# Gated linear attention, output stage: two heads on the partitions, both directions in the free dimension, and masks applied by one multiplication

## The chip, the cores and the metric

The kernel runs on one core of a Trainium2 chip. The metric is device time in microseconds (us), the median of three runs. The engines are called as in the profile: PE (TensorE), DVE (VectorE), ACT (ScalarE), POOL (GpSimd) and SP (SyncE, which issues the DMAs).

## The reference

Two layers over 2048 latent tokens and 256 context tokens, model width 1024. Layer 0 has latent attention and an mLSTM; layer 1 has a bidirectional gated linear attention (GLA, 4 heads, key width 64, value width 128) and a 2-D neighbourhood attention (8 heads). The change touches the GLA alone. For one head and one direction, cut to what matters:

```python
bcum = jnp.cumsum(gc, axis=2)                      # gc: log decay per token and key channel
rel = bcum[:, :, :, None, :] - bcum[:, :, None, :, :]
decay = jnp.exp(jnp.where(causal[:, :, None], rel, -jnp.inf))
att = jnp.einsum('bhtd,bhsd,bhtsd->bhts', qc, kc, decay)
o = att @ vc + (qc * jnp.exp(bcum)) @ S            # S: state before the chunk
```

The second direction runs over the flipped sequence, and the outputs of both directions are added. Then a per-head RMS norm follows.

## The kernel before

Layer 1 first makes one projection, a long row of f16 products on PE (`gemm_in`: L322 with 384 columns where tokens stand in the columns, L343 with 256 columns where they stand on the rows). It is split into parts, and the parts of the GLA are written between them: gates (`gla_gates`, L1126), chunk states (`gla_state`, L1186), projection of q, `gla_out` (L1262), the projection for the neighbourhood attention, and that attention (`na_attn`). A scheduler orders each engine's instructions for the whole program before it is built; each engine then runs its list in order. So the products of the projection stand between the products of `gla_out`, and fill PE while the GLA waits.

`gla_out` goes over 16 chunks of 128 tokens. The decay between two tokens of a chunk is not formed token by token. For block sizes hb = 64, 32, 16 (HIGH) and 8, 4, 2, 1 (LOW), `decay` subtracts from the summed log decay its value at the middle of each block of 2·hb tokens (`Dt`, POOL, L1301), and takes the exponential of both halves with opposite signs (`E`, ACT, L1303 and L1304, into PSUM). Queries of one half times keys of the other half, each multiplied by `E`, then give the products between the two halves of a block.

The partitions hold direction times 64 key channels, and the free dimension holds the 4 heads. So one direction's queries are the first half of a block and the other's are the second half, on other partitions, and each level needs `queries` twice with 64 partitions (DVE, L1308, L1309), and for HIGH also the keys twice (L1321, L1322). For LOW the keys are multiplied whole (L1333), and `R` and `Sb` hold zeros where nothing may count. HIGH products are added up in one PSUM tile, `pb` (L1327). LOW products go to places of their own (`pl`, L1342) in 32 by 32 blocks, the diagonal too (L1344, in a second tile `o`). ACT copies `pb` to `att` and the first LOW level to `ac`. DVE then takes from each level what its mask allows:

```python
nc.vector.copy_predicated(ac, mkc[:, li - 1, None, :]..., pc[:, li] if li < len(LOW) else o[:, :, 0:32])
nc.vector.copy_predicated(att, mkx[...], ac[...])
```

Last come `att` times `v` (L1355) and the queries `qe` times the state `Z` (L1356), the squares for the norm on ACT (L1358), a copy (`ob`, L1360) and a store. `E` has two buffers in PSUM, `pb` and `o` share two, `pl` has one.

A float32 product of the program is two matmuls in the trace. A product with 32 or 64 output rows takes only a strip of PE's array: the forms 128\*32 and 128\*64 in the profile are rows times columns of the part of the array that is used.

Of the kernel before, what the change touches and what calls it, by code (L numbers as in the profile page):

```python
# [7 lines left out]
F32 = mybir.dt.float32  # L8
# [4 lines left out]
U32 = mybir.dt.uint32  # L13
AF = mybir.ActivationFunctionType
ALU = mybir.AluOpType
AX = mybir.AxisListType
PSUM = bass.MemoryType.PSUM
# [41 lines left out]
class Kern:  # L59
# [1066 lines left out]
    def gla_gates(self, kp):  # L1126
# [4 lines left out]
        with tc.tile_pool(name="gl_gc", bufs=1, side="right") as gc, tc.tile_pool(name="gl_g", bufs=2, side="right") as gp, \  # L1131
# [24 lines left out]
            for g in (0, 2):  # L1156
# [11 lines left out]
                for a in range(2):  # L1168
# [6 lines left out]
                    nc.sync.dma_start(S["glB"][:, h], Fp[:, h])  # L1175
# [86 lines left out]
    def gla_out(self):  # L1262
        nc, tc, I, S = self.nc, self.tc, self.I, self.S
        HIGH, LOW = (64, 32, 16), (8, 4, 2, 1)
        with ExitStack() as es:
# [5 lines left out]
            pl = mk(name="gl_pl", bufs=1, space=PSUM)  # L1271
            po = mk(name="gl_po", bufs=2, space=PSUM)
            mkc = cp.tile([P, 4, 32], F32, name="mkc")
            nc.sync.dma_start(mkc, I["lmaskc"].rearrange("l s t -> s l t"))
            mkx = cp.tile([P, 4, 32], F32, name="mkx")
            nc.sync.dma_start(mkx, I["lmaskx"].rearrange("s (n t) -> s n t", t=32))
            Sb = cp.tile([P, len(HIGH), 4, P], F32, name="Sb")
            nc.gpsimd.memset(Sb, 0.0)
            R = []
            for i in range(2):  # L1280
                r = cp.tile([P, len(HIGH + LOW), 4, P], F32, name=f"R{i}")
                nc.gpsimd.memset(r, 0.0)
                R.append(r)
            def load(c):
                cs = slice(c * P, (c + 1) * P)
                t = [lp.tile([P, 4, P], F32, name=n, bufs=b) for n, b in (("B", 3), ("q", 2), ("k", 2), ("v", 2), ("Z", 3))]
                B, q, k, v, Z = t
                nc.sync.dma_start(B, S["glB"][:, :, cs])
                for r in (0, 64):
                    nc.sync.dma_start(k[r:r + 64], S["gk"][:, cs].rearrange("(h p) t -> p h t", p=64))  # L1290
                    nc.sync.dma_start(q[r:r + 64], S["gq"][:, cs].rearrange("(h p) t -> p h t", p=64))
                nc.sync.dma_start(v, S["gva"][cs, 0:512].rearrange("p (h d) -> p h d", h=4))
                nc.sync.dma_start(Z[0:64], S["glZ"][c, 0:64])
                nc.sync.dma_start(Z[64:128], S["glZ"][NT + 1 - c, 64:128])
                return t

            def decay(hb, B):
                F = lambda t: t.rearrange("p h (n x) -> p (h n) x", x=2 * hb)
                V = lambda t: t.rearrange("p h (n s b) -> p (h n) s b", s=2, b=hb)
                Dt = wp.tile([P, 4, P], F32, name="Dt")  # L1300
                nc.gpsimd.tensor_tensor(F(Dt), F(B), F(B)[:, :, hb:hb + 1].broadcast_to([P, 4 * P // (2 * hb), 2 * hb]), ALU.subtract)  # L1301
# [3 lines left out]
                return V, E  # L1305

            def queries(V, E, q, r):
                nc.vector.tensor_tensor(V(r)[0:64, :, 1], V(E)[0:64, :, 1], V(q)[0:64, :, 1], ALU.mult)  # L1308
                nc.vector.tensor_tensor(V(r)[64:128, :, 0], V(E)[64:128, :, 0], V(q)[64:128, :, 0], ALU.mult)  # L1309

            order = [c for i in range(NT // 2, 1, -1) for c in (i, NT + 1 - i)]
            nxt = load(order[0])
            for i, c in enumerate(order):
                B, q, k, v, Z = nxt
                nxt = load(order[i + 1]) if i + 1 < len(order) else None
                Rc = R[c % 2]
                pb = po.tile([P, 4, P], F32, name="o")
                for li, hb in enumerate(HIGH):
                    V, E = decay(hb, B)
                    Sv = V(Sb[:, li])  # L1320
                    nc.vector.tensor_tensor(Sv[0:64, :, 0], V(E)[0:64, :, 0], V(k)[0:64, :, 0], ALU.mult)  # L1321
                    nc.vector.tensor_tensor(Sv[64:128, :, 1], V(E)[64:128, :, 1], V(k)[64:128, :, 1], ALU.mult)  # L1322
                    queries(V, E, q, Rc[:, li])
                    for h in range(4):
                        for n in range(P // (2 * hb)):
                            w = slice(n * 2 * hb, (n + 1) * 2 * hb)
# [469 lines left out]
```

## Time and profile before

| what | us |
| --- | --- |
| median of 3 runs | 3649.45 (3647.62 to 3654.1) |
| the profiled execution | 3645.0 |
| its span, first to last instruction | 3642.7 |
| PE busy | 3391.9 (93%) |
| DVE busy | 2563.9 (70%) |
| ACT busy | 1832.6 (50%) |
| POOL busy | 972.9 (27%) |

The span leaves 2.3 us of the profiled execution around it. Busy time counts an engine as busy from the start to the end of each instruction. Matmuls are pipelined, and the next begins before the last has ended, so for PE the distance between starts says more than the durations. A wait is put down to the instruction whose signal came last.

### The profile page before, as it was taken

The numbers are of one execution on the slowest core, as the hardware profiler recorded it, in microseconds if no ns is written. First come the engines' busy times: TensorE is split into PE (matmuls) and PEld (weight loads), VectorE is DVE, ScalarE is ACT, GpSimd is POOL, SyncE is SP. The second block draws the span as 40 slices with busy tenths as digits, with TensorE's granted clock in tenths as the row PEclk, the third lists the DMA queues.
The fourth block names the chain that finished last, engine by engine and source line by source line (L and its number), as shares of the span: only waits on it lengthen the run. The fifth ranks groups of instructions, "written<-read, shape, count | busy, mean of one in ns | idle before, by whom it ended". The sixth has DMA issues, their size and how long they took to land.

```text
span 3642.7 us, 77364 instructions
## 1 busy us (share of the span) xinstructions
PE 3391.9 (93%) x30588; PEld 2575.3 (71%) x30588; DVE 2563.9 (70%) x5697; ACT 1832.6 (50%) x3243; POOL 972.9 (27%) x908
## 2 busy tenths in 40 slices
PE   6999999999888899999999999999888899899898
PEld 3566888898556677777777555676565789898754
DVE  5657576678766888888887566354688547776887
ACT  4333323334443577777777433256465435455632
POOL 1012204473221233333333222101355322111122
PEclk8999999999999799999999999999999999999999
DMA  7632347776778222221110543227554545437343
GB/s 264 242 122 69 141 179 227 222 234 218 215 225 231 77 49 52 53 49 47 31 47 14 168 152 121 66 83 211 166 160 133 144 98 145 123 96 194 117 164 122
DMA packets 400535, 498.35 MB, mean 137 GB/s; under 512 B 104110, under 2 KB 306339, under 8 KB 394988
## 3 DMA queue, kind: packets, MB, share of 16 engines
q1 hardware_dynamic: 400172, 493.40, 44.7%
q8 instruction: 241, 3.95, 0.5%
q14 instruction: 122, 1.00, 0.1%
HBM read 311.73 MB, written 181.43 MB: 135 GB/s over the span
## 4 chain that ended last, share of the span: by engine, by line
PE 58%; DVE 20%; DMA 12%; issue 5%; ACT 4%; POOL 1%; SPq 1%; POOLq 0%; DVEq 0%; ACTq 0%
PE ps L343 13%; PE ps L322 8%; PE po L633 5%; PE ops L1119 4%; PE pm L578 4%; PE ps L613 3%; PE ps L615 3%; PE ps L614 3%; PE t L1544 2%; DVE mc L579 1%; PE s L1522 1%; PE o L1560 1%; PE s L1523 1%; DMA scr_mqkc<-y 1%; PE ps L489 1%
## 5 line engine op out<-in xcount | busy, mean ns | idle before, releaser
L343 PE MATMUL ps<-wh,uh 128*128 128x256 f16 (+3 forms) x2816 | 742.6, 269 | 33.8 <-ACT ot L278 13.0
L343 PE MATMUL ps<-wl,uh 128*128 128x256 f16 (+3 forms) x2816 | 741.6, 268 | 0.0
L343 PE MATMUL ps<-wh,ul 128*128 128x256 f16 (+3 forms) x2816 | 736.3, 268 | 1.4 <-POOL ul L210 1.4
L343 PEld LDWEIGHTS <-uh 128*128 128x128 f16 x5632 | 532.1, 99 | 118.2 <-issue 43.4
L579 DVE TENSOR_REDUCE mc<-pm 128x1 f32<-128x512 f32 (+1 forms) x656 | 403.2, 628 | 115.5 <-PE pm L578 107.3
L618 ACT ACTIVATE p<-ps 128x1024 f32<-128x1024 f32 (+1 forms) x296 | 299.8, 1013 | 158.8 <-PE ps L615 119.2
L322 PE MATMUL ps<-uh,wh 128*128 128x384 f16 (+2 forms) x1008 | 323.9, 325 | 7.5 <-DVE ofs L332 2.8
L322 PE MATMUL ps<-ul,wh 128*128 128x384 f16 (+2 forms) x1008 | 326.1, 326 | 1.1 <-DVE ul L210 1.1
L322 PE MATMUL ps<-uh,wl 128*128 128x384 f16 (+2 forms) x1008 | 325.7, 325 | 0.0
L622 POOL TENSOR_TENSOR pl<-p,ph 128x1024 f16<-128x1024 f32 (+1 forms) x98 | 207.9, 2122 | 434.8 <-ACT ph L619 416.5
L619 ACT CAST ph<-p 128x1024 f16<-128x1024 f32 (+1 forms) x296 | 306.4, 1035 | 7.6
L343 PEld LDWEIGHTS <-ul 128*128 128x128 f16 x2816 | 277.6, 99 | 37.7 <-POOL ul L210 2.6
L322 PEld LDWEIGHTS <-wh 128*128 128x128 f16 (+1 forms) x2016 | 198.2, 100 | 134.8 <-issue 24.0
L578 PE MATMUL pm<-kk,qq 96*128 96x512 f32 (+1 forms) x656 | 271.5, 418 | 21.4 <-DVE mc L579 15.8
L622 DVE TENSOR_TENSOR pl<-p,ph 128x1024 f16<-128x1024 f32 (+1 forms) x198 | 244.4, 1236 | 27.7 <-ACT ph L619 23.0
L301 POOL TENSOR_TENSOR wl<-wr,wh 128x2048 f16<-128x2048 f32 (+4 forms) x31 | 121.3, 3914 | 492.8 <-ACT wh L300 431.0
L633 PE MATMUL po<-v,ph 128*128 128x129 f16 x2336 | 246.8, 221 | 0.0
L613 PE MATMUL ps<-qq,kk 96*128 96x512 f32 (+1 forms) x592 | 240.5, 406 | 0.0
L633 PEld LDWEIGHTS <-pl 128*128 128x128 f16 x2336 | 196.6, 98 | 61.2 <-issue 58.9
L633 PE MATMUL po<-v,pl 128*128 128x65 f16 x2336 | 237.4, 194 | 0.4 <-DVE pl L622 0.4
L615 PE MATMUL ps<-qq,kk 98*128 98x512 f32 (+1 forms) x592 | 233.1, 394 | 0.0
L614 PE MATMUL ps<-qq,kk 96*128 96x512 f32 (+1 forms) x592 | 232.4, 393 | 0.0
(429 smaller groups left out, 7997.3 us busy)
## 6 DMA issues: line engine op xcount, KB each, us to landing
wr<-in_l_w_in_dram SPq DMA_DIRECT2D x26, 1024.0 KB
wm<-in_l_w_mod_dram SPq DMA_DIRECT2D x12, 2048.0 KB
z<-scr_z SPq DMA_DIRECT2D x34, 512.0 KB
scr_z<-ot SPq DMA_DIRECT2D x44, 384.0 KB
k<-scr_nk SPq DMA_DIRECT2D x14, 1152.0 KB
scr_mqk<-of SPq DMA_DIRECT2D x48, 192.0 KB
x<-scr_mqk SPq DMA_DIRECT2D x8, 1152.0 KB
scr_mqkc<-y SPq DMA_DIRECT2D x8, 1152.0 KB
```

Of the source, the lines that this page charges most:

```text
L322: nc.tensor.matmul(ps[0:m, t0:BLK], w_[:, k, m0:m0 + m], u_[:, k, t0:BLK], start=(q == 0), stop=(q == 3 * KT - 1))
L343: nc.tensor.matmul(ps[:, 0:n], u_[:, k, i * P:(i + 1) * P], w_[:, k, 0:n], start=(q == 0), stop=(q == 3 * KT - 1))
L578: nc.tensor.matmul(pm[:, 0:n], qq[0:96, 0, s * P:(s + 1) * P], kk[0:96, 0, u * 512:u * 512 + n], start=True, stop=True)
L579: nc.vector.reduce_max(mc[:, s, u:u + 1], pm[:, 0:n], AX.X)
L613: nc.tensor.matmul(pj[:, 0:nq], kk[0:96, 0, ks], qq[0:96, 1, 0:nq], start=True, stop=False)
L614: nc.tensor.matmul(pj[:, 0:nq], kk[0:96, 1, ks], qq[0:96, 0, 0:nq], start=False, stop=False)
L615: nc.tensor.matmul(pj[:, 0:nq], kk[0:98, 0, ks], qq[0:98, 0, 0:nq], start=False, stop=True)
L618: nc.scalar.activation(p32[:, :, 0:nq], ps[:, :, 0:nq], AF.Exp, scale=scale)
L619: nc.scalar.copy(ph[:, :, 0:nq], p32[:, :, 0:nq])
L622: eng.tensor_tensor(pl[:, :, 0:nq], p32[:, :, 0:nq], ph[:, :, 0:nq], ALU.subtract)
L633: nc.tensor.matmul(o_, p_[:, j, s * P:(s + 1) * P], v[:, kt, 0:w], start=w == 129 and kt == 0 and s % 2 == 0, stop=w == 129 and kt == kts[ ...
L1119: nc.tensor.matmul(ps, c_[:, k], w_[k][:, ns], start=(q == 0), stop=(q == 3 * KT - 1))
```

## The change

In `gla_out` the partitions now hold two heads times 64 key channels, and the free dimension holds the two directions and the other factor two of the heads. The two halves of a block are then at different places of the free dimension, and one access pattern, `pick`, takes for both directions the half that each needs. So each level needs one DVE instruction for the keys and one for the queries. A product now sums over 64 partitions, one head; the directions are two products that add up in PSUM, and the two heads on the partitions (`r`) go to two PSUM tiles. HIGH levels 64 and 32 multiply only the quarter that is not zero.

LOW comes first. Its four levels and the diagonal lie beside each other in `pc[r]`; one DVE multiplication per `r` with the mask (L1362, the diagonal's mask is 2 since it was counted once for each direction before) leaves `m0` and `m1`. Products with the identity add the five parts up at their place in `ps[r]`, and the HIGH levels are added onto them. ACT copies the sum to `att0` and `att1`. The output goes to the other half of the same PSUM tile. Four PSUM tiles a chunk share three buffers. `mm` (L1329) makes each product of a chunk stand behind the last one that began a sum. The scratch tensor `glB` changes its layout, so `gla_gates` stores two halves for each head.

```diff
-                    nc.sync.dma_start(S["glB"][:, h], Fp[:, h])
+                    for d in range(2):
+                        nc.sync.dma_start(S["glB"][h % 2 * 64:h % 2 * 64 + 64, d, h // 2], Fp[d * 64:d * 64 + 64, h])
...
-            pl = mk(name="gl_pl", bufs=1, space=PSUM)
-            po = mk(name="gl_po", bufs=2, space=PSUM)
+            po = mk(name="gl_po", bufs=3, space=PSUM)
...
-            def queries(V, E, q, r):
-                nc.vector.tensor_tensor(V(r)[0:64, :, 1], V(E)[0:64, :, 1], V(q)[0:64, :, 1], ALU.mult)
-                nc.vector.tensor_tensor(V(r)[64:128, :, 0], V(E)[64:128, :, 0], V(q)[64:128, :, 0], ALU.mult)
...
+                def mm(out, l, r, start=False, stop=True):
+                    with tc.issue_after(head[0].ins) if head[0] is not None else ExitStack():
+                        x = nc.tensor.matmul(out, l, r, start=start, stop=stop, skip_group_check=True)
...
+                    nc.vector.tensor_tensor(pick(St, hb, 0), pick(E[:], hb, 0), H(k), ALU.mult)
+                    nc.vector.tensor_tensor(pick(Rt, hb, 1), pick(E[:], hb, 1), H(q)[:, ::-1], ALU.mult)
+                    m = 2 * hb if high else 32
+                    for h in range(2):
+                        for a in range(2):
+                            for n in range(P // m):
...
+                                for r in range(2):
+                                    rs = slice(r * 64, r * 64 + 64)
+                                    mm(out(r, w, h, x), St[rs, 2 * a + h, w], Rt[rs, 2 * a + h, x], hb == LOW[0] and h == a == 0)
...
+                    nc.vector.tensor_tensor(m5, pc[r][:, 0:320].rearrange("p (l h t) -> p l h t", l=5, h=2), mk5[:, :, None].broadcast_to([P, 5, 2, 32]), ALU.mult)
...
+                    for n in range(4):
+                        w = slice(n * 32, n * 32 + 32)
+                        for l in range(5):
+                            mm(pb[w, :, w], self.ident[:, w], pm[r][:, l], l == 0)
...
-                for li in range(1, len(LOW) + 1):
-                    nc.vector.copy_predicated(ac, mkc[:, li - 1, None, :].broadcast_to([P, 4, 32]).bitcast(U32), pc[:, li] if li < len(LOW) else o[:, :, 0:32])
-                nc.vector.copy_predicated(att, mkx[:, None].broadcast_to([P, 4, 4, 32]).bitcast(U32), ac[:, :, None, :].broadcast_to([P, 4, 4, 32]))
...
+                        mm(o, att[r][:, h * P:(h + 1) * P], v[:, 2 * h + r], h == 0, False)
+                        for a in range(2):
+                            mm(o, qe[rs, a, h], Z[rs, a, h], False, a == 1)
```

On PE, before, the output products of one chunk stand among the LOW products of the next (`R` and `Sl`, `pl`), behind a run of the projection (L322):

```order
L322 MATMUL ps<-ul_27711,wh 128x384
L1342 MATMUL pl<-R_31263,Sl 32x32 x24
L1355 MATMUL o<-v,att 128x128
L1356 MATMUL o<-Z,qe 128x128
...
L1342 MATMUL pl<-R_31263,Sl 32x32 x40
L1344 MATMUL o<-q,k 32x32 x16
```

After the change, PE has three runs a chunk, with about 22, 22 and 16 products of the projection between them: LOW and the diagonal, then what is shown first here (identity, HIGH, and one first product of the next chunk), then the output:

```order
L1329 MATMUL o<-m_31473,ident 32x2x32 x20
L1329 MATMUL o<-m_31475,ident 32x2x32 x20
L1329 MATMUL o<-X_31263 64x64 x8
L1329 MATMUL o<-X_31263 32x32 x16
L1329 MATMUL o<-R_31264,S_31266 32x32 x32
L1329 MATMUL o<-R_31269,S_31271 32x32
...
L1329 MATMUL o<-v,att_31596 128x128
L1329 MATMUL o<-Z,qe 128x128 x2
```

The number of products of the stage on PE goes from 1856 to 4032 (two matmuls each in the trace), and of each 20 identity products five that follow each other go to the same strip.

On DVE, before, the two masks of a chunk stand among the levels of the next:

```order
L1333 TENSOR_TENSOR Sl<-E,k 128x512
L1308 TENSOR_TENSOR R_31263<-E,q 64x32x8
L1309 TENSOR_TENSOR R_31263<-E,q 64x32x8
L1348 COPY_PREDICATED ac<-mkc,pl 128x128 x3
L1348 COPY_PREDICATED ac<-mkc,o 128x128
L1349 COPY_PREDICATED att<-mkx,ac 128x512
L1333 TENSOR_TENSOR Sl<-E,k 128x512
L1308 TENSOR_TENSOR R_31263<-E,q 64x64x4
```

After it, the mask products `m` of a chunk stand behind all seven levels of the next chunk (`X`, `S`, `R`), and ahead of the levels of the one after that:

```order
L1338 TENSOR_TENSOR S_31271<-E,k 128x2x8x16
L1339 TENSOR_TENSOR R_31269<-E,q 128x2x8x16
L332 SCALAR_TENSOR_TENSOR ofs<-ps,wes,ofs 128x384
L306 SCALAR_TENSOR_TENSOR wes<-wsc,us 128x1
...
L290 TENSOR_REDUCE wmx<-wr 128x1 x4
L1362 TENSOR_TENSOR m_32151<-o,mk_31258 128x320
L1362 TENSOR_TENSOR m_32153<-o,mk_31258 128x320
L291 TENSOR_REDUCE wmx<-wmx 128x1
L1338 TENSOR_TENSOR S_31266<-E,k 128x2x16x8
```

The levels have moved a whole chunk ahead of the products that read them.

## Rows read from the trace of the kernel before

**Rows 1.** The page, part 1: busy us, share of the span, instructions.
```profile
PE 3391.9 (93%) x30588; PEld 2575.3 (71%) x30588; DVE 2563.9 (70%) x5697; ACT 1832.6 (50%) x3243; POOL 972.9 (27%) x908
```
**Rows 2.** First and last matmul of the stage: count, ns min/median/max, first to last start.
```profile
L1327 PE MATMUL o<-R,Sb x896: 196/217/552, 2599.4 to 2857.7; 128*32 128x32 f32 x103, 128*64 128x64 f32 x51, 128*128 128x128 f32 x26
L1356 PE MATMUL o<-Z,qe x128: 275/275/422, 2626.1 to 2879.7; 128*128 128x128 f32 x128
```
**Rows 3.** Busy us in the stretch: PE, PEld, DVE, ACT, POOL; clock, DMA share, GB/s.
```profile
2599.00:2880.00 281.00, 239.55 (x4563) 174.09 (x4564) 235.63 (x531) 165.70 (x490) 147.81 (x133) 0.95 0.48 145
```
**Rows 4.** Groups by line, 2590 to 2881: count, busy us, mean ns, idle before.
```profile
L1309 DVE TENSOR_TENSOR R<-E,q 64x256 f32<-64x256 f32 x112 | 47.8, 428 | 1.9
L1308 DVE TENSOR_TENSOR R<-E,q 64x256 f32<-64x256 f32 x112 | 46.0, 411 | 1.0
L1333 DVE TENSOR_TENSOR Sl<-E,k 128x512 f32<-128x512 f32 x64 | 43.9, 686 | 4.6 <-ACT E L1304 3.7
L1322 DVE TENSOR_TENSOR Sb<-E,k 64x256 f32<-64x256 f32 x48 | 20.5, 427 | 1.0
L1321 DVE TENSOR_TENSOR Sb<-E,k 64x256 f32<-64x256 f32 x48 | 19.7, 413 | 10.1 <-ACT E L1304 9.5
L1349 DVE COPY_PREDICATED att<-mkx,ac 128x512 f32<-128x512 uint32 x16 | 19.6, 1224 | 0.4
L1348 DVE COPY_PREDICATED ac<-mkc,pl 128x128 f32<-128x128 uint32 x48 | 14.4, 300 | 3.5 <-ACT ac L1346 2.3
L1348 DVE COPY_PREDICATED ac<-mkc,o 128x128 f32<-128x128 uint32 x16 | 4.8, 299 | 0.8
L1301 POOL TENSOR_TENSOR Dt<-B 128x512 f32<-128x512 f32 x112 | 120.0, 1079 | 86.3 <-ACT E L1304 72.0 <-DMA B<-scr_glB 8.1 <-issue 3.2
```
**Rows 5.** Waits, 2590 to 2881: us in total, times, longest us.
```profile
PEld o L1355 <- DVE att L1349: 17.4, 9, 3.5
PEld pl L1342 <- DVE R L1309: 9.6, 13, 1.2
PEld o L1327 <- DVE R L1309: 5.3, 8, 1.6
...
ACT E L1303 <- DVE R L1309: 75.5, 64, 6.9
POOL Dt L1301 <- ACT E L1304: 72.0, 63, 5.9
```
**Rows 6.** PE in order of time: start us, us, line, form, count.
```profile
2704.31 0.39 PE L1355 MATMUL o<-v,att 128*128 128x128 f32 x2
2704.53 0.39 PE L1356 MATMUL o<-Z,qe 128*128 128x128 f32 x2
2704.85 0.28 PE L1327 MATMUL o<-R,Sb 128*32 128x32 f32 x9
2704.94 0.21 PE L1342 MATMUL pl<-R,Sl 128*32 128x32 f32 x3
2704.97 0.20 PE L1327 MATMUL o<-R,Sb 128*32 128x32 f32 x1
2704.97 1.18 PE L1342 MATMUL pl<-R,Sl 128*32 128x32 f32 x93
...
2707.66 0.46 PE L1342 MATMUL pl<-R,Sl 128*32 128x32 f32 x32
2708.09 0.46 PE L1344 MATMUL o<-q,k 128*32 128x32 f32 x32
2708.48 0.34 PE L322 MATMUL ps<-uh,wl 128*128 128x384 f16 x1
...
2711.90 0.33 PE L322 MATMUL ps<-uh,wl 128*128 128x384 f16 x1
...
2879.93 0.27 PE L343 MATMUL ps<-wh,uh 128*128 128x256 f16 x1
...
2881.02 0.27 PE L343 MATMUL ps<-wl,uh 128*128 128x256 f16 x1
```

More of the change, by code (lines that the diff above doesn't have):

```diff
@@ L1315, in gla_out @@
                 nxt = load(order[i + 1]) if i + 1 < len(order) else None
-                Rc = R[c % 2]
-                pb = po.tile([P, 4, P], F32, name="o")
-                for li, hb in enumerate(HIGH):
[L1319 to L1326, printed above, removed]
-                            nc.tensor.matmul(pb[w, h, w], Sb[:, li, h, w], Rc[:, li, h, w], start=(li == 0 and h == 0), stop=True, skip_group_check=True)
@@ L1328, in gla_out @@
-                att = wp.tile([P, 4, 4, 32], F32, name="att", bufs=1)
-                nc.scalar.copy(att, pb.rearrange("p h (n t) -> p h n t", t=32))
-                Sl = wp.tile([P, len(LOW), 4, P], F32, name="Sl")
-                for li, hb in enumerate(LOW):
-                    V, E = decay(hb, B)
-                    nc.vector.tensor_tensor(Sl[:, li], E, k, ALU.mult)
-                    queries(V, E, q, Rc[:, len(HIGH) + li])
-                pc = pl.tile([P, len(LOW), 4, 32], F32, name="pl")
@@ L1336, in gla_out @@
-                o = po.tile([P, 4, P], F32, name="o")
-                for li in range(len(LOW) + 1):
-                    for h in range(4):
-                        for n in range(4):
-                            w = slice(n * 32, (n + 1) * 32)
-                            if li < len(LOW):
-                                nc.tensor.matmul(pc[w, li, h], Sl[:, li, h, w], Rc[:, len(HIGH) + li, h, w], start=(li == 0 and h == 0), stop=True, skip_group_check=True)
-                            else:
-                                nc.tensor.matmul(o[w, h, 0:32], k[:, h, w], q[:, h, w], start=(h == 0), stop=True, skip_group_check=True)
@@ new lines, in gla_out @@
+                pc = [po.tile([P, 512], F32, name="o") for _ in range(2)]
+                for l, hb in enumerate(LOW):
+                    level(l + len(HIGH), hb, lambda r, w, h, x: pc[r][w, l * 64 + h * 32:l * 64 + h * 32 + 32])
+                for h in range(2):
+                    for n in range(4):
+                        w = slice(n * 32, n * 32 + 32)
+                        for r in range(2):
+                            rs = slice(r * 64, r * 64 + 64)
+                            mm(pc[r][w, 256 + h * 32:288 + h * 32], k[rs, h, w], q[rs, h, w])
@@ new lines, in gla_out @@
+                for li, hb in enumerate(HIGH):
+                    level(li, hb, lambda r, w, h, x: ps[r][w, h * P + x.start:h * P + x.stop])
+                att = []
+                for r in range(2):
+                    at = wp.tile([P, 256], F32, name=f"att{r}")
+                    nc.scalar.copy(at, ps[r][:, 0:256])
+                    att.append(at)
+                qe = wp.tile([P, 2, 2, P], F32, name="qe")
+                nc.scalar.activation(qe[:, 0], B[:, 0], AF.Exp, scale=1.0 / 16)
```

104 lines of the change are left out of this document (65 added, 39 removed).

## The prediction

> **What bounds the stage now.** I read the page first: PE is busy for 93% of the span [rows 1], so work added to PE costs time wherever it stands, and work taken from another engine pays only where PE waits for it. The change touches one stage, so I looked for its ends: the first matmul of `gla_out` starts at 2599.4 and the last at 2879.7 [rows 2]; with 0.3 us for the last, the stage takes 280.6 us. In this stretch DVE is busy for 235.6 of 281 us, PE for 239.6, ACT for 165.7 and POOL for 147.8 [rows 3].
>
> Next, the waits. PE waits for DVE: 17.4 us before `att`, 9.6 and 5.3 before `R` [rows 5]. ACT waits 75.5 us for `R`, since DVE has not yet freed one of the two `E` buffers, and POOL 72.0 us for ACT [rows 5]. So ACT and POOL wait for DVE, and the DVE instructions of a level have nearly no idle time ahead of them (1.9, 1.0, 1.0 us over the stage) [rows 4]. DVE sets the pace of the GLA here, and PE fills its waits with the projection.
>
> How much of PE's time is waiting? Busy time doesn't tell, since matmuls overlap, so I take distances between starts. An L322 matmul: 21 steps from 2708.48 to 2711.90, 0.163 us. L343: 10 steps from 2879.93 to 2881.02, 0.109 us. Float32 with 128 columns: two pairs from 2704.31 to 2704.53, 0.11 us each. On 32-wide strips, four taken in turn: 32 matmuls end after 0.46 us and one alone lasts 0.20, so 0.26/31 = 0.0084 us. A change of form costs about 0.10 us: the pair of 2704.53 should be followed at 2704.75 and is at 2704.85; the 32 of 2708.09 need 0.27 us, and the next form starts after 0.39 [rows 6].
>
> In the order, 691 L322 and 149 L343 matmuls stand between the stage's first and last: 112.6 + 16.2 = 128.8 us. The stage's own products are two matmuls each: 384 with 128 columns (42.2 us), 256 with 64 (half of 0.11 us, two strips side by side, about 0.03: 7.7) and 3072 with 32 (25.8), 75.7 us. I count 124 changes of form, 12.4 us. Sum 216.9; so 63.7 of 280.6 us are waits. These are what the change can win.
>
> **DVE.** Removed: L1308, L1309, L1333, L1321, L1322, L1348 (two rows) and L1349, 216.7 us in sum [rows 4]. Added: 14 products of 128x256 a chunk and two of 128x320. An instruction with 256 elements on 64 partitions takes 0.43 us, one with 512 on 128 partitions 0.69 [rows 4], so 256 on 128 lie between half of that, 0.34, and 0.43; I take 0.43, the same length. For 320 I take 0.49, between 0.43 and 0.69. 16 x (14 x 0.43 + 2 x 0.49) = 112 us. DVE falls from 235.6 to about 131 of 281 us, and no longer sets the pace.
>
> **PE.** By the order, the number of products goes from 1856 to 4032. At the price of rows:
>
> - 64 rows by 32 columns, 3072 products, 6144 matmuls. No row shows strips of half the rows. If the upper and lower halves run side by side, half of 0.0084: 25.8 us. If they take turns, double: 103 us. I take 0.007 (43.0 us), near the row of the same width, a little below, because the first three of another form start within 0.01 us [rows 6], at 2704.94.
> - 64 by 64, 256 matmuls: between 0.015 and 0.03, 3.8 us taken, 7.7 at most.
> - Identity, 128 by 32, 64 columns, 1280 matmuls. Alone on its strip one takes half of 0.11, 0.055: 70.4 us. With four strips side by side a quarter: 17.9 us. Five that follow each other go to one strip, so it depends on whether PE takes later ones ahead. A row says that it can: of `R`, whose five products stand ahead of `pl` in the order, the tenth matmul starts at 2704.97, after three of `pl` that began at 2704.94 [rows 6]. I take 0.02, 25.6 us.
> - `qe` times `Z` is now two products where there was one: 256 x 0.11 = 28.2 us (14.1 before). They share one half of the rows and follow each other, so I grant no overlap. `att` times `v` stays at 14.1 us.
> - 229 changes of form, 22.9 us, above all between `att` times `v` (128 rows) and `Z` (64 rows), eight times a chunk.
>
> Sum 137.6 us for 88.1 before: PE gets 49.5 us more to do. The order puts 285 L343 matmuls into the stage and not 149; those are taken from behind it, so I compare with the same 128.8 us of projection.
>
> The Trainium skill, "TensorE: Matmul & The Clock Gate", section "Wait — 56ns, not 53.3ns?", states that starts are never nearer than about 25 ns. By it the 6144 matmuls would cost 154 us and the change would be 111 us worse than I forecast. The trace disagrees, with 8.4 ns here, so it gets no chance.
>
> **What is left of the waits.** After the change PE has three runs a chunk, and the projection between them covers what they wait for. LOW's end to the masks: 22 L322, 3.6 us, for two products of 0.49. From LOW's end DVE then runs the masks and seven levels of a later chunk, and ACT's copy to `att` stands behind the exponentials of those levels, which wait for DVE's buffers: 2 x 0.49 + 14 x 0.43 = 7.0 us, and about a third more for the exponentials and evictions that DVE then waits for, an estimate: 9.2 us. Its cover is 44 L322 (7.2 us) and the run of identity and HIGH (about 3): enough, by 1 us. In the last five chunks the cover is L343, 4.8 + 3, and 1.5 us a chunk are late, 7.5 us. The first chunk has nothing ahead of it; I give it 5 us. Waits that have nothing to do with DVE (weights of the projection, DMAs) I put at 7. So 20 us of 63.7 stay.
>
> ACT and POOL lose little and have time: 165.7 and 147.8 of 281 us. Loads get fewer pieces for `q` and `k` and more for `Z`; all are asked for a chunk ahead. The two tiny loads of `br` and the larger clearing of `R` and `S` on POOL stand ahead of the stage, beside the projection: nothing. The three buffers for four tiles make LOW wait for the copy of the first output tile; 16 matmuls of projection (2.6 us) cover it.
>
> **Sum.** 128.8 + 137.6 + 20 = 286.4 us, against 280.6: 5.8 us longer. The profiled execution took 3645.0 us (span 3642.7 and 2.3 around it), 4.5 below the median; put onto the median of 3649.45, that gives 3655. A difference below 0.2%, 7.3 us, can't be told from none.
>
> **Rivals.**
>
> 1. Faster: half-row strips run side by side, and the identity products overlap. 25.8 and 22 us in place of 43.0 and 25.6, and 15 us of waits: 260.6, 20 us less than before, 3629. For it: four column strips do run side by side. Against it: no row has half the rows, and starts nearer than 0.007 us are nowhere seen.
> 2. Slower: the identity products run one after another. It is one loop, `n` outside and `l` inside; it decides once PE does not look past about 10 matmuls for another strip. 70.4 in place of 25.6, with 6 us less waiting since the longer run covers the copies: +38.8 on the forecast, 3694. For it: the row shows PE going three ahead, no further.
>  By the Trainium skill, the same page, section "Part 3: Packing small matmuls — row/col tiling", matmuls start strictly in program order, which gives this case. The row at 2704.97 speaks against the rule, at short distance.
> 3. Half-row strips of one column strip take turns: 103 in place of 43.0, 3715. Against it: the two heads go to different PSUM tiles.
> 4. The waits stay: with three buffers for four tiles a chunk, and `m` behind seven levels on DVE, PE waits as long as before, 63.7 us: +43.7 on the forecast, 3699. Against it: DVE has 150 us of room.
>
> **Chances.** Forecast 0.42, rival 1 0.28, rival 2 0.20, rival 3 0.06, rival 4 0.04. The forecast's own range is about 12 us to each side (3643 to 3667): of its 0.42, 0.06 are faster by more than 7.3 us, 0.17 within, 0.19 slower. Rival 1 is faster but for 0.03; the other three are slower. Together: faster 0.31, same 0.20, slower 0.49. The range from 3624 to 3697 holds the forecast, most of rival 1 and rival 2.
>
> **What would show it.** The span from the first to the last matmul of the stage near 300 us (286 and the 14 us of projection that move in). DVE near 130 us in it. PE's waits for DVE near nothing before the output products. The 32-wide products at 0.007 us a start, an identity run of 40 products within 1.6 us: 0.055 a matmul, 4.4 us, would mean rival 2, and 0.004 for the 32-wide ones rival 1. I am wrong if PE still waits for `m` or `att` in most chunks, or if DVE's products on 128 partitions take clearly more than 0.43 us.

## The result, and the profile after

The changed kernel takes 3763.6 us (median of 4 runs, 3759.9 to 3766.8), the kernel before, run beside it, 3651.8 (3647.6 to 3661.6). The ratio is 1.0309, 95% interval 1.0294 to 1.0325: 112 us slower. The forecast was 3655, its range ended at 3697, and none of its rivals reached the time.

The page's parts 1 and 3, of the changed kernel (part 1 as in [rows 1]; part 3: packets, MB, share of the DMA engines):

```profile
PE 3492.8 (93%) x34940; PEld 2658.4 (71%) x34940; DVE 2463.7 (66%) x5489; ACT 1823.7 (49%) x3243; POOL 971.5 (26%) x909
...
q8 instruction: 274, 4.49, 0.5%
```

PE has 4352 matmuls and as many weight loads more, DVE is busy for 100 us less. In q8 a packet is 4.49 MB / 274 = 16 KB of instructions.

The line that now issues all products of the stage (as in [rows 2], below it what its engine waited for, us and times):

```profile
L1329 PE MATMUL o<-R,S x5120: 186/193/260, 2602.7 to 2997.8; 64*32 64x32 f32 x197
...
L1329 PE MATMUL o<-Z,qe x256: 272/272/373, 2628.1 to 3004.5; 64*128 64x128 f32 x128
...
its engine sat idle before it (us, times) until:
  issue: 81.0, 56
  DVE R L1339: 7.8, 6
```

The stage takes 402 us, 121 more than before [rows 2]. The second thing to see is "issue": PE and its load side, which overlap, waited 81 us in sum for nothing that the profile names. The same stretch as [rows 3]:

```profile
2602.00:3005.00 403.00, 356.08 (x9046) 269.15 (x9047) 135.86 (x333) 160.56 (x501) 145.41 (x142) 0.94 0.30 94
```

DVE fell from 235.6 to 135.9 us. PE is busy for 116 us more, and still idle for 46.9 us, 41.4 before. DVE's groups that took the place of [rows 4]:

```profile
L1338 DVE TENSOR_TENSOR S<-E,k 128x256 f32<-128x256 f32 x80 | 32.6, 421 | 41.5 <-DMA k<-scr_gk 23.0 <-ACT E L1315 16.0 <-issue 2.4
L1339 DVE TENSOR_TENSOR R<-E,q 128x256 f32<-128x256 f32 x80 | 32.2, 416 | 0.8 <-DMA q<-scr_gq 0.6
...
L1362 DVE TENSOR_TENSOR m<-o,mk 128x320 f32<-128x320 f32 x32 | 14.2, 486 | 91.0 <-PE o L1329 91.0
L1338 DVE TENSOR_TENSOR X<-E,k 128x256 f32<-128x256 f32 x32 | 13.5, 421 | 15.2 <-PE o L1329 12.5 <-ACT E L1315 2.8
L1339 DVE TENSOR_TENSOR X<-E,q 128x256 f32<-128x256 f32 x32 | 13.3, 415 | 0.0
```

The sum is 105.8 us. The large idle time has changed sides: DVE waits 91 us for PE before the masks. The waits of PE, as in [rows 5]:

```profile
PEld o L1329 <- issue: 44.0, 37, 5.5
PE o L1329 <- issue: 37.1, 19, 5.4
...
PEld o L1329 <- DVE R L1339: 3.9, 3, 3.0
```

The waits for DVE are gone but for 3.9 us, and the waits for `issue` stand in their place. PE in order of time, as in [rows 6], with the idle time before a row in brackets:

```profile
2717.80 1.11 PE L1329 MATMUL o<-R,S 64*32 64x32 f32 x107 [1.33 <-issue]
2718.76 0.32 PE L1329 MATMUL o<-q,k 64*32 64x32 f32 x21
2721.93 0.35 PE L1329 MATMUL o<-q,k 64*32 64x32 f32 x11 [2.85 <-issue]
...
2801.41 3.30 PE L1329 MATMUL o<-m,ident 128*32 128x64 f32 x80
2804.64 0.75 PE L1329 MATMUL o<-X 64*64 64x64 f32 x48
...
2809.70 0.39 PE L1329 MATMUL o<-v,att 128*128 128x128 f32 x2
2810.01 0.71 PE L1329 MATMUL o<-Z,qe 64*128 64x128 f32 x4
2810.65 0.49 PE L1329 MATMUL o<-v,att 128*128 128x128 f32 x2
...
2811.70 0.49 PE L1329 MATMUL o<-v,att 128*128 128x128 f32 x2
```

Look at 2717.80 to 2721.93: between two stops lie 107 + 21 = 128 matmuls, with their loads some 256 instructions. The stops stand in the middle of a run, with no other engine named. Counted in the trace, more than 0.4 us passed from one start on PE or its load side to the next, put down to `issue`, 22 times in the stage, 45.5 us in all. From 2695 on the distances between stops are 255, 510, 1020 or 1275 instructions, give or take one: one, two, four or five times the same block. In the stage before I count 8 such stops, 9.4 us. What the queue of instructions moved in this stage, and below it in the stage before:

```profile
q8 instruction: 72, 1.18, 1.2%
...
q8 instruction: 37, 0.61, 0.9%
```

72 packets stand beside PE's 18093 matmuls and loads, 251 for each packet; in the stage before it was 37 for 9127, 247. So a packet of 16 KB is such a block, but for the few that belong to other engines.

The packets also stand at the stops. In the stop that ends at 2721.93 lies one of them (the view of 2719.2 to 2721.9):

```profile
q8 instruction: 1, 0.02, 2.0%
```

By the trace's list of packets it has landed at 2720.59, and PE goes on 1.34 us later. Each of the 22 stops ends 1.2 to 1.6 us after such a landing. Of the 8 stops in the stage before only the two longest do, 2.8 and 2.4 us. The longer one cuts a run of `pl`:

```profile
2802.86 0.38 PE L1342 MATMUL pl<-R,Sl 128*32 128x32 f32 x11 [2.57 <-issue]
```

The other six don't, nor do 32 of the 33 waits of over 0.4 us there that other engines ended. So six of the 8 were something else, and the changed kernel has 22 stops for instructions where the kernel before had two.

The clock around the longest stop, 2664.7 to 2670.0 (columns as in [rows 3], the granted clock is the third number from the right):

```profile
2661.00:2666.00 5.00, 3.66 (x265) 2.93 (x264) 0.62 (x1) 0.64 (x2) 1.27 (x1) 1.00 0.83 249
2666.00:2671.00 5.00, 0.97 (x29) 0.60 (x29) 2.90 (x6) 0.00 (x0) 0.00 (x0) 0.58 0.70 200
2671.00:2676.00 5.00, 5.00 (x24) 2.72 (x23) 1.93 (x7) 0.83 (x3) 0.00 (x0) 0.73 0.20 56
2676.00:2681.00 5.00, 5.00 (x198) 4.48 (x197) 2.89 (x8) 2.39 (x7) 4.20 (x4) 1.00 0.16 58
```

The mean is 0.58 in the row that holds most of the stop and 0.73 in the next: after PE came to stand the clock fell from 2.4 to 1.2 GHz, and the first products of the projection behind the stop run at the lower level. So a stop costs more than its length. In this one the DMA engines were busy with data (0.83 and 0.70 of the two rows), and the packet of instructions began 2.6 us after PE's last start. The stage's groups on PE (count, busy us, mean ns, idle before):

```profile
L1329 PE MATMUL o<-R,S 64*32 64x32 f32 x5120 | 60.8, 204 | 29.4 <-issue 24.6 <-DVE R L1339 3.9 <-POOL Dt L1312 0.9
L1329 PE MATMUL o<-m,ident 128*32 128x64 f32 x1280 | 52.9, 222 | 0.0
L1329 PE MATMUL o<-Z,qe 64*128 64x128 f32 x256 | 45.4, 297 | 0.0
L1329 PE MATMUL o<-v,att 128*128 128x128 f32 x128 | 29.6, 313 | 0.0
L1329 PE MATMUL o<-q,k 64*32 64x32 f32 x512 | 8.5, 222 | 12.6 <-issue 12.4
L1329 PE MATMUL o<-X 64*64 64x64 f32 x256 | 7.4, 230 | 0.0
L1329 PE MATMUL o<-X 64*32 64x32 f32 x512 | 6.0, 198 | 0.1
```

They are busy for 210.6 us; the seven groups of the stage before sum to 128.9.

### The profile page after: what moved, and what is told of

It reads as the page before. It is cut to its first block, busy times and chain, and to the rows that moved or that the text cites. A ratio compares the mean times of both kernels' runs of the same rounds, so it can differ in the third digit from the quotient of the medians.

```text
span 3757.8 us, 85860 instructions
## 1 busy us (share of the span) xinstructions
PE 3492.8 (93%) x34940; PEld 2658.4 (71%) x34940; DVE 2463.7 (66%) x5489; ACT 1823.7 (49%) x3243; POOL 971.5 (26%) x909
## 3 DMA queue, kind: packets, MB, share of 16 engines
q8 instruction: 274, 4.49, 0.5%
## 4 chain that ended last, share of the span: by engine, by line
PE 63%; DVE 15%; DMA 11%; issue 5%; ACT 3%; POOL 1%; SPq 1%; POOLq 0%; DVEq 0%; ACTq 0%
PE ps L343 13%; PE ps L322 10%; PE o L1329 5%; PE po L633 5%; PE ops L1119 4%; PE pm L578 3%; PE ps L613 3%; PE ps L615 3%; PE ps L614 3%; PE t L1577 2%; DVE mc L579 1%; PE s L1555 1%; PE o L1593 1%; PE s L1556 1%; PE po L976 1%
## 5 line engine op out<-in xcount | busy, mean ns | idle before, releaser
L343 PE MATMUL ps<-wh,uh 128*128 128x256 f16 (+3 forms) x2816 | 746.0, 270 | 34.9 <-ACT ot L278 13.5
L343 PE MATMUL ps<-wl,uh 128*128 128x256 f16 (+3 forms) x2816 | 744.3, 269 | 0.2 <-issue 0.2
L343 PE MATMUL ps<-wh,ul 128*128 128x256 f16 (+3 forms) x2816 | 739.7, 269 | 1.9 <-POOL ul L210 1.9
L343 PEld LDWEIGHTS <-uh 128*128 128x128 f16 x5632 | 533.8, 99 | 121.3 <-issue 44.6
L322 PE MATMUL ps<-uh,wh 128*128 128x384 f16 (+2 forms) x1008 | 327.0, 328 | 5.6 <-DVE wmx L291 2.7
L322 PE MATMUL ps<-ul,wh 128*128 128x384 f16 (+2 forms) x1008 | 329.0, 328 | 3.1 <-issue 1.7
L322 PE MATMUL ps<-uh,wl 128*128 128x384 f16 (+2 forms) x1008 | 328.4, 328 | 0.0
L343 PEld LDWEIGHTS <-ul 128*128 128x128 f16 x2816 | 278.6, 99 | 39.5 <-POOL ul L210 2.9
L322 PEld LDWEIGHTS <-wh 128*128 128x128 f16 (+1 forms) x2016 | 199.4, 101 | 137.0 <-issue 26.6
```

The lines of the kernel that those rows point to most:

```text
L322: nc.tensor.matmul(ps[0:m, t0:BLK], w_[:, k, m0:m0 + m], u_[:, k, t0:BLK], start=(q == 0), stop=(q == 3 * KT - 1))
L343: nc.tensor.matmul(ps[:, 0:n], u_[:, k, i * P:(i + 1) * P], w_[:, k, 0:n], start=(q == 0), stop=(q == 3 * KT - 1))
```

## The experiments

Theory A: in a long run of short matmuls PE uses up its instructions faster than they come, and stands still for the next block. Rival B: half-row strips are slow in PE's array. Rival C: three PSUM buffers and DVE's order make the waits. The kernel before was run beside each experiment. Differences between experiments are taken from their ratios to it, at 3649 us. "Stops" are counted as above: over 0.4 us from one start on PE or its load side to the next, on `issue`, in the stage.

**1. Short matmuls doubled on the old layout.** In the kernel before:

```diff
-                for li in range(len(LOW) + 1):
+                for li, rep in [(x, y) for x in range(len(LOW) + 1) for y in range(2)]:
```

> The kernel before, with each product of the four small levels and of the diagonal issued twice (128 rows by 32 columns; what is added up is then double in these parts). It has 5120 such matmuls, near the 6144 of the changed kernel, but on all 128 rows, and every other engine works as before. Theory A (PE runs out of fetched instructions in a long run of short matmuls: in the changed kernel it stands still 22 times for 45.5 us with nothing to wait for, at distances that are multiples of 255 of its instructions, and blocks of 16 KB come no nearer than 3.5 us): the same stops appear in this kernel inside the doubled runs, 10 to 20 of them, and the stage grows by 40 to 70 us. Rival B (the half-row strips are what is slow): the 2560 added matmuls take the 8.4 ns of the kernel before, 21 us in all, with no more stops than before (3). Rival C (three PSUM buffers and DVE's order make the waits): as B.

3707.3 us, ratio 1.0160 (1.0138 to 1.0183): 58 us slower, 23 ns for each added matmul with its load, where B had 21 us in all. A's 40 to 70 us were meant for the stage. The stage itself grew by 7 us only: it holds 336 fewer products of the projection, and these follow behind it. There are 26 stops, 48.0 us (A: 10 to 20). The two groups in the profile of this kernel:

```profile
L1342 PE MATMUL pl<-R,Sl 128*32 128x32 f32 x4096 | 49.2, 204 | 21.2 <-issue 17.1 <-DVE R L1309 3.6 <-DVE ac L1348 0.4
L1344 PE MATMUL o<-q,k 128*32 128x32 f32 x1024 | 15.5, 210 | 20.8 <-issue 19.1 <-ACT att L1329 1.7
```

`issue` makes 36 of their 42 us of idle time. Nothing of the change is in this kernel but the number of matmuls, so neither half rows nor the buffers are needed for the stops.

**2. The same, four times** (`range(4)` in that line).

> The kernel before with each product of the four small levels and of the diagonal issued four times (these parts are then four times as large): 7680 matmuls and as many weight loads more than before. With each issued twice it was 58.3 us slower, 22.8 ns an added matmul. Theory A: PE takes its instructions at 13.7 ns each in a long run (blocks of 256 come 3.5 us apart), 27 ns a load and matmul, so 175 to 210 us slower. Rival B: 8.4 ns a matmul, 65 us, on top of the 37 us of stops seen with two: about 100.

3858.0 us, ratio 1.0576 (1.0558 to 1.0594): 210 us slower for 7680 pairs of matmul and load, 27.4 ns a pair, the upper end of A's range. 63 stops, 140.6 us. In order of time, and the stage in one row:

```profile
2706.39 2.27 PE L1342 MATMUL pl<-R,Sl 128*32 128x32 f32 x200
2711.78 1.93 PE L1342 MATMUL pl<-R,Sl 128*32 128x32 f32 x128 [3.12 <-issue]
2715.25 0.98 PE L1342 MATMUL pl<-R,Sl 128*32 128x32 f32 x56 [1.54 <-issue]
```
```profile
2601.00:2976.00 375.00, 247.20 (x11465) 220.78 (x11466) 202.21 (x463) 140.50 (x458) 131.09 (x123) 0.67 0.25 72
```

Here is the block: a run of 128 matmuls, then a stop, and from its start to the next start 3.47 us, 27 ns a pair. (The nearest two packets in the stage of the changed kernel start 3.3 us apart, a little less than the 3.5 us that the expectations take.) PE is busy for 66% of the stretch and idle for the rest, and the clock's mean is 0.67. Inside a run the array still starts a matmul each 14 ns or faster. So this rate isn't the array's. 60 of the 63 stops end 1.2 to 1.6 us after a packet of q8 has landed. Traffic beside them isn't needed: of the stops behind a single block, 32 had next to no data moving (under three packets) and lasted 2.1 us in the mean, 11 had a hundred packets or more and lasted 2.5.

**3. Identity products on four strips in turn.** In the changed kernel:

```diff
-                    for n in range(4):
-                        w = slice(n * 32, n * 32 + 32)
-                        for l in range(5):
+                    for l in range(5):
+                        for n in range(4):
+                            w = slice(n * 32, n * 32 + 32)
```

> The changed kernel with the two loops of the identity products exchanged, so that neighbours go to four different column strips and not five to one. The 1280 identity matmuls take 38.9 ns each in the changed kernel, 49 us. If one strip at a time is the cause, they fall to 15 to 20 ns and the kernel gains 20 to 30 us. Theory A says that a part of it comes back as waits for instructions, since the same number is issued in less time: a gain of 5 to 20 us. If the 38.9 ns are already a wait for instructions (27 ns a load and matmul), nothing changes (within 5 us).

3762.5 us, ratio 1.0313 (1.0298 to 1.0329), as the changed kernel. Yet the identity products themselves got faster:

```profile
L1329 PE MATMUL o<-R,S 64*32 64x32 f32 x5120 | 61.0, 204 | 35.0 <-issue 30.9 <-DVE R L1339 2.7 <-POOL Dt L1312 1.3
...
L1329 PE MATMUL o<-m,ident 128*32 128x64 f32 x1280 | 21.3, 221 | 0.0
```
```profile
2612.00:3006.00 394.00, 333.91 (x9048) 240.90 (x9046) 137.34 (x331) 159.79 (x498) 144.27 (x141) 0.91 0.31 96
```

52.9 became 21.3 us. In return there are 28 stops, 56.7 us; PE's idle time in the stage is 60.1 us for 46.9, and the clock 0.91 for 0.94, which is 11 us more lost to the lower level (394 x 0.09 for 403 x 0.06). 31.6 us were won and some 24 are seen to come back. The time is that of the last case in the expectation, but not for its reason, since the matmuls did get faster; A had the right reason and too small a price (it left a gain of 5 to 20). The slow identity run seems to have been time in which instructions could catch up. In the profiled execution the stage is 8 us shorter, as these numbers say, but it also began 10 us later. The part ahead of it, which the edits hardly touch, differs that much between executions (the profiled stages begin at 2592.9 to 2612.6), so a difference of a few us is read from the medians alone, and they show no gain.

**4. Masked parts summed on DVE**, so that a chunk has 8 identity products and not 40:

```diff
+                    ms = wp.tile([P, 2, 32], F32, name=f"ms{r}", bufs=1)
+                    nc.vector.tensor_reduce(ms, m5.rearrange("p l h t -> p h t l"), AX.X, ALU.add)
...
-                        for l in range(5):
-                            mm(pb[w, :, w], self.ident[:, w], pm[r][:, l], l == 0)
+                        mm(pb[w, :, w], self.ident[:, w], pm[r], True)
```

> The changed kernel with the five masked parts summed on DVE (one reduction of 128x320 to 128x64 a tile, 32 in all, about 0.5 us each, 16 us of DVE), so that a chunk has 8 identity products and not 40: 1024 matmuls and their loads fewer. Theory A: 40 us of identity matmuls go, and the runs of LOW, identity and HIGH are 128 instructions shorter a chunk, so that some of the 45.5 us of stops go too: 35 to 60 us faster than the changed kernel. Rival B: the 40 us only. Rival C (DVE late with m): the reduction makes m later by 0.5 us a tile, and the gain is under 25 us.

3742.8 us, ratio 1.0253 (1.0231 to 1.0275), 20 us less than the changed kernel. A's 35 to 60 missed: it took the stops to fall, and they rose, to 31 and 62.8 us. Rival C's number fits, but not its reason: PE doesn't wait for the sums, it waits for instructions.

```profile
L1329 PE MATMUL o<-R,S 64*32 64x32 f32 x5120 | 61.7, 205 | 42.2 <-issue 38.3 <-DVE R L1339 3.7
```

1024 pairs fewer gave 20 us: 20 ns a pair, as if the time in the array didn't count.

**5. Output products in groups**: the four of `att` and `v`, then the eight of `qe` and `Z`, halves in turn.

```diff
-                        mm(o, att[r][:, h * P:(h + 1) * P], v[:, 2 * h + r], h == 0, False)
-                        for a in range(2):
-                            mm(o, qe[rs, a, h], Z[rs, a, h], False, a == 1)
+                        mm(ps[r][:, (2 + h) * P:(3 + h) * P], att[r][:, h * P:(h + 1) * P], v[:, 2 * h + r], h == 0, False)
+                for h in range(2):
+                    for a in range(2):
+                        for r in range(2):
+                            mm(ps[r][:, (2 + h) * P:(3 + h) * P], qe[rs, a, h], Z[rs, a, h], False, a == 1)
```

> The changed kernel with the output products in another order: first the four of att and v (128 rows), then the eight of qe and Z (64 rows), the two halves taken in turn. Changes between 128 and 64 rows fall from eight to two a chunk. Theory: a matmul of att and v takes 187 ns from start to start there and the change back 205 ns, for 112 ns without a change; 6 fewer changes a chunk at 0.1 to 0.2 us are 10 to 19 us, and 256 Z matmuls whose neighbours use different halves of the rows may overlap (28 us now, 14 if they do): 10 to 30 us faster than the changed kernel. Rival: the output run waits for att and for the copies of the first half, which now come later: no gain (within 5 us).

3749.4 us, ratio 1.0266 (1.0240 to 1.0291), 16 us less than the changed kernel, as expected. On PE itself more was won:

```profile
L1329 PE MATMUL o<-R,S 64*32 64x32 f32 x5120 | 59.7, 204 | 50.4 <-issue 46.2 <-DVE R L1339 2.9 <-POOL Dt L1312 0.9
...
L1329 PE MATMUL o<-Z,qe 64*128 64x128 f32 x256 | 19.3, 286 | 0.0
L1329 PE MATMUL o<-v,att 128*128 128x128 f32 x128 | 17.0, 276 | 0.0
```

75.0 us of output products became 36.3. Two things changed at once, the number of turns between 128 and 64 rows and the halves taken in turn, and they weren't tried apart. The stops went to 25 and 56.1 us. The stage is hardly shorter, 401 us, but holds 142 more L343 products, so the gain shows behind it.

**6. Both edits** (4 and 5).

> Both edits that helped the changed kernel: the five masked parts summed on DVE (alone 20.8 us less) and the output products in groups (alone 14.2 us less). If they add up, 35 us less than the changed kernel, about 3728. Theory A: part of what they save is waited for again, since the same instructions of LOW now stand closer together: 3728 to 3745. In either case clearly slower than the kernel before, since the 6144 matmuls of 64 rows and their loads are still there.

3706.0 us, ratio 1.0156 (1.0142 to 1.0170): 56 us less than the changed kernel, more than the 36 of the two alone and below A's range. Stops 22, 57.6 us. A had them eat a part of the gain; they don't grow on from where edit 4 alone had left them. PE's idle time in the stage says the same: 46.9 us in the changed kernel, 60.2 and 56.1 with one edit, 60.0 with both. Each edit alone pays for its gain with idle time; together they pay once.

**7. Half the instructions.** In the changed kernel, tiles R, S and X in bfloat16:

```diff
-                r = [cp.tile([P, 2, 4, P], F32, name=f"X{i}")]
+                r = [cp.tile([P, 2, 4, P], BF16, name=f"X{i}")]
...
-                    t = cp.tile([P, 5, 4, P], F32, name=f"{n}{i}")
+                    t = cp.tile([P, 5, 4, P], BF16, name=f"{n}{i}")
```

> The changed kernel with the decayed q and k of all seven levels (tiles R, S and X) kept in bfloat16, so that a product is one matmul and one weight load where it was two of each; their values are rounded, the rest is computed as before. 2944 matmuls and as many loads fewer. The 2944 matmuls take about 10 ns from start to start in the changed kernel, 29 us. Theory A (PE runs out of instructions): the run of LOW with the diagonal falls from about 576 to about 320 instructions, the 22 stops of 45.5 us fall to under 15 us too, and the kernel gains 50 to 75 us. Rival B (array time of half-row strips alone): 25 to 35 us, the stops staying where they are.

3699.2 us, ratio 1.0146 (1.0132 to 1.0160): 59 us less than the changed kernel, in A's range, 20 ns for each pair left out. 13 stops, 18.7 us (A: under 15), and no `issue` before the products of R and S:

```profile
L1329 PE MATMUL o<-R,S 64*32 64x32 bf16 x2560 | 28.9, 182 | 5.1 <-DVE R L1339 5.1
```

**8. The exchange of 3 again, with bfloat16.**

> The kernel with decayed q and k in bfloat16, and the two loops of its identity products exchanged. The same exchange gained nothing in the changed kernel (3762.5 for 3763.6), where it took the identity matmuls from 38.9 to 13.9 ns, 31 us, and the stops for instructions grew by 11 us. Theory A (the gain was eaten because PE's instructions were the limit): with half the instructions in LOW it comes through here, 15 to 30 us less than the 3699 of the kernel with bfloat16 alone. Rival (something else is waited for after the identity products): again nothing, within 5 us.

3688.6 us, ratio 1.0118 (1.0103 to 1.0134): 10 us less than 7. It does gain here and didn't in 3, but less than A's 15 to 30: the stops go back up to 19 and 29.1 us. So 7 isn't free of the shortage; its slow identity run was still cover.

**9. All of 4, 5 and 7.**

> The changed kernel with the decayed q and k in bfloat16, the parts summed on DVE and the output products in groups. Alone the first gained 64.4 us and the other two together 57.7. Theory A: the stops that these two could still remove are mostly gone by the first, so that the sum of 122 us isn't reached; what they save of PE's own time, 44 us of identity matmuls and 31 us of output products and changes of form, stays: 3620 to 3645, faster than the kernel before. If the two edits' gain was mostly stops, about 3660.

3653.6 us, ratio 1.0015 (1.0003 to 1.0027). A's 3620 to 3645 missed by 9 us, and the kernel isn't faster than the one before; the time lies between the two figures of the expectation. 11 stops, 11.5 us. What is late now:

```profile
L1329 PE MATMUL o<-v,att 128*128 128x128 f32 x128 | 21.5, 321 | 20.5 <-ACT att L1377 20.4
```

With PE's runs shorter, ACT's copy to `att`, behind the exponentials of later levels, is what PE waits for.

**10. Control: the kernel before in bfloat16** (R, Sb and Sl).

> A control: the kernel before with its decayed q and k (R, Sb and Sl) in bfloat16, nothing else changed. Its 3200 matmuls of levels become 1600 and its 384 of 128 columns 192 (one in three forms), some 40 us of PE's work less, but DVE keeps its 235.6 us of the stage's 281 and sets the pace. The stage can't be shorter than DVE's work: 0 to 30 us less than the kernel before, and PE's waits for DVE longer than their 32 us.

3622.0 us, ratio 0.9934 (0.9916 to 0.9952), 24 us faster than the kernel before: the lowest median here, on the old layout and with DVE as busy as ever:

```profile
2611.00:2896.00 285.00, 249.95 (x3437) 176.74 (x3438) 244.41 (x551) 174.01 (x509) 150.47 (x148) 0.95 0.51 149
```

The waits for DVE didn't get longer, as I had expected (its 17.4 us before `att` are 10.1). PE's shorter work lets it take more projection between the runs (its L343 products in the stage went from 151 to 494), so the gain shows behind the stage, which is no shorter (284 us).

**11. The mask half alone, on the old layout.** In the kernel before:

```diff
-                nc.scalar.copy(ac, pc[:, 0])
-                for li in range(1, len(LOW) + 1):
-                    nc.vector.copy_predicated(ac, mkc[...], ...)
-                nc.vector.copy_predicated(att, mkx[...], ac[...])
+                nc.vector.tensor_tensor(ac[:, 0:4], pc, mk5[...], ALU.mult)
+                nc.vector.tensor_tensor(ac[:, 4], o[:, :, 0:32], mk5[...], ALU.mult)
+                for l in range(5):
+                    for n in range(4):
+                        nc.tensor.matmul(pb[w, :, w], self.ident[:, w], ac[:, l], start=False, ...)
```

> The other half of the change on the layout of the kernel before (one head on 128 rows, both directions on the partitions): one multiplication by masks and 20 identity products a chunk in place of the five predicated copies, and no half-row strips. DVE loses 38.8 us of predicated copies and gains 16 us of masks; PE gets 640 matmuls of 128 columns, on four strips in turn about 0.028 us each, 18 us, and 80 instructions more a chunk. Theory A: its runs stay short, the stops for instructions stay below 15 us and the time is between 10 us less and 20 us more than the kernel before. Rival (the masks are what made the change slow): 30 us or more slower.

3663.3 us, ratio 1.0038 (1.0025 to 1.0051): 14 us slower, in the range. So the masks account for 14 of the 112 us at most; that the rest comes with the layout is a subtraction, since the layout was not run without the masks. The identity products, four strips in turn, and the stops that are left (5, 11.0 us):

```profile
L1347 PE MATMUL o<-ac,ident 128*32 128x128 f32 x640 | 20.8, 275 | 0.0
...
L1340 PE MATMUL o<-q,k 128*32 128x32 f32 x512 | 8.5, 203 | 7.8 <-issue 7.1 <-ACT ob L1360 0.5
```

**12. The same with the sum on DVE** (one reduction, 4 identity products a chunk).

> As the one with the masks alone, with the five parts summed by one reduction on DVE (about 1 us for 128x640), so that a chunk has 4 identity products and not 20: PE gets 128 matmuls, about 4 us. DVE loses 38.8 us and gains about 32. att now waits for masks, reduction, identity and copy in a row, about 1.5 us a chunk longer than before. Expected within 10 us of the kernel before, and faster than the one without the reduction if PE's instructions are what is short.

3655.9 us, ratio 1.0007 (0.9994 to 1.0021): not told from the kernel before, as expected, 11 us less than 11.

**13 and 14. Both mask kernels with bfloat16.**

> The kernel before with decayed q and k in bfloat16 (alone 25.5 us faster) and with the mask half of the change (alone 14 us slower): two multiplications by masks and 20 identity products a chunk in place of the predicated copies. If what the masks cost is PE's own time for 640 identity matmuls (17 us), they cost nearly the same here: 3630 to 3640. If it was instructions in short supply, they fit now, and DVE's 20 us less pay: 3605 to 3620.

> As the one before it, with the five parts summed on DVE and 4 identity products a chunk (in float32 this cost 7 us and is hardly told from no change). PE's own time grows by 4 us only. DVE, which sets the pace here, loses about 7 us net, but att waits for masks, reduction, identity and copy in a row: 3610 to 3630.

3627.7 us (0.9955, 0.9940 to 0.9969) and 3626.2 us (0.9940, 0.9927 to 0.9954). The first fell just short of its 3630 to 3640, with one stop of 1.4 us, before the stage's first load: where instructions are enough, the masks with 640 identity matmuls still cost 8 us by the ratios, which speaks for PE's own time. With the sum on DVE they cost 2, within the uncertainty. In no kernel did the mask half gain.

## Why the prediction was wrong

**DVE: right.** 105.8 us for a forecast of 112, 135.9 for 131 in the stage; 0.42 us for 128x256 (0.43 taken), 0.486 for 128x320 (0.49).

**The step that failed: "What is left of the waits ... So 20 us of 63.7 stay."** The waits for DVE did go. But the step knew only waits for other engines. Each run on PE has to be supplied with instructions too, and LOW with the diagonal grew from 160 to 288 matmuls on end with as many loads, more than two blocks. PE's idle time was to fall by 43.7 us and rose by 5.5. The kernel before had shown it in small: two stops for instructions, one of them at 2802.86 in the middle of a run of `pl`; I took `issue` for noise.

The 63.7 us were themselves too much. They are what single distances, taken at the full clock, left over of the stage, but PE is idle there for 41.4 us (281.00 less 239.55 in [rows 3]): 43.7 could not be won from that. Counted in the trace over the whole stage, by all distances between starts with the waits of over 0.4 us taken out, the own products took 103 us and not 88.1, the projection 137 and not 128.8.

**Terms mis-sized.** PE's own products were to grow by 49.5 us. They grew by 81.7 busy us, and by 91, from 103 to 194, in the forecast's own measure, distances between starts.
- 64 by 32: inside a run (107 in 1.11 us, the last lasting 0.2) 8.6 ns, 7 taken; with breaks 60.8 + 8.5 + 6.0 us busy, 43.0 forecast. The half rows neither take turns (rival 3) nor run side by side (rival 1).
- Identity: 25.6 forecast, 52.9 measured, 80 matmuls in 3.2 us: 40 ns, between the forecast's 20 and rival 2's 55. As rival 2 had it, the order of the loop decides: four strips in turn need 21.3 (experiment 3), so PE didn't reach past ten matmuls for another strip. But alone it doesn't move the time.
- Output: 42.3 us and 12.8 of changes of form forecast, 75.0 measured: a head takes 1.05 us (2810.65 to 2811.70), not 0.86.

The rest of the miss is the projection, 162 us by distances where 143 were counted. It shares the lower clock: the mean fell from 0.95 to 0.94 over a longer stretch, 24 us lost to the lower level in place of 14.

**The sum.** The stage was to grow by 20 us, projection included, and grew by 121. Of the 101 between, 49 are idle time (5.5 more, not 43.7 less), 41 own products (91 more, not 49.5) and 11 the projection (25 more, not 14); what the lower clock cost is contained in the last two.

**The rule that got no chance.** The Trainium skill, "TensorE: Matmul & The Clock Gate", section "Wait — 56ns, not 53.3ns?", has starts never nearer than about 25 ns, and my estimate from it was 111 us beyond the forecast. The time came out 109 us beyond it. My reason against it stands as far as it goes: starts 8.6 ns apart are in this trace too, inside a run. What I missed is that a rate inside a short run is no rate for a long one. Over several blocks a pair costs 27 ns here, near the rule's figure, but the rows show another cause than a limit on single starts: 128 pairs quickly, and then a stop. The agreement of the two numbers is partly luck, since identity and output terms were off as well.

**An account by pairs**, an estimate: short matmuls (32 or 64 columns out of a strip) went from 3328 to 7680 in the stage. At the 20 to 27 ns that a pair cost in experiments 1, 2, 4 and 7, 4352 more are 87 to 119 us; 112 were measured. Experiments 4 and 7, which took pairs out of the changed kernel, gave 20 ns each. Those that made matmuls faster without taking any out gave nothing (3), 10 us (8) and 16 us (5), each less than PE's own saving. The estimate isn't a proof: waits for other engines fell too, from 38 us in the kernel before to 18 and 2 in experiments 1 and 2 and 5 in the changed kernel, so a pair's price is what is left after that.

**Rival 4** had its number (3699) from waits for DVE, and that is not what happened; three buffers played no part that the rows show. Its mechanism came up only in experiment 9, as the copy to `att`.

That the stops are waits for blocks of instructions is shown by the number of instructions (1, 2, 7), by the distances of 256 and by the packets that land 1.2 to 1.6 us before each stop ends. Where little else moved they were shorter, not absent (experiment 2). What decides when a packet begins stays open: in the 22 stops it was from 2.2 us before PE's last start to 2.6 us after it.

## What to carry to other kernels

Count instructions on an engine as a resource of its own: where runs of short matmuls are longer than a block (256 instructions here; runs of 320 instructions had two stops for them in the stage, runs of 576 had 22), price a matmul with its load by the long run (27 ns here) and not by the distance of starts inside it (8 ns). A layout that relieves a busy second engine by splitting products on PE pays twice for them, in PE's own time and in instructions, and a profile shows the second as idle time put down to `issue` in the middle of a run, at distances that are multiples of one block. When a large saving on one group of instructions doesn't move the time, look whether idle time of another kind grew by as much, as in experiment 3.

## What was not expected of the hardware

- PE's instructions come in packets of 16 KB, 256 of them; in the longest runs a new block is used up each 3.5 us, and where PE waits for it, it starts 1.2 to 1.6 us after the packet has landed.
- In the 5 us that held most of a stop of 5.5 us the granted clock was 0.58, in the next 5 us 0.73, then 1.00. Over the stage its mean fell with the stops: 0.95 before (9.4 us), 0.91 with 56.7 us, 0.67 with 140.6 us.
- Matmuls that follow each other on one strip of 32 columns (128 rows, 64 columns moved) start 40 ns apart; four strips in turn, 17 ns by busy time.
- Output products that turn from 128 rows to 64 and back at each head took 75.0 us; in two groups, with the halves of the rows in turn, 36.3.
